# Output projection of a hybrid decoder block: when its loads are asked for, on which queue, and into which PSUM banks

## The chip, the cores and the metric

One core of a Trainium2 chip runs the whole program. The metric is device time in microseconds of one execution. Three runs of the kernel before gave 2572.22 (median), 2565.59 and 2573.88 us.

## The reference, cut to what matters

The block has 2048 tokens of width 1024, all in f32. The part that this change touches sits between the mixer's attention and the MLP:

```python
# hybrid_mixer: four gated-linear-attention heads (go), four differential-attention heads (do)
do = diff_attention(dq, dk, dv, lam)
do = from_heads(rms_norm(do, diff_norm) * (1.0 - lambda_init))
y  = jnp.concatenate([go, do], axis=-1) @ w_out          # the output projection
# reference
x = x + gt_a * rms_norm(y, post_norm_mix[l])              # residual add
h = rms_norm(x, pre_norm_mlp[l]) * (1.0 + sc_m) + sh_m    # what the MLP reads
y = jnp.square(jax.nn.relu(h @ w_up[l])) @ w_down[l]
```

## The kernel before, in words

Every f32 matrix product is made from three passes over halves: high times high, high times low, low times high. The tokens are 16 tiles of 128 rows; four tiles form a block t of 512 rows.

**Attention** (generator `attention`, lines 175 to 335) runs in two sweeps, blocks 0 and 1 first, blocks 2 and 3 second. One of its steps makes scores S for 512 keys (PSUM tag "C"), VectorE moves them out (L223, L226), ScalarE takes the exponent (L236), TensorE transposes P into PT (tag "C" too), and the product with V collects in O (tag "D"). When all four query tiles of a head and block are in, `norm` (L283) scales them into `don`, and `finish` (L296) transposes them (dps, L301), splits them into high and low halves (dmo, L303 and L304) and stores them with GpSimd's DMA queue into mixS in DRAM (L306). `finished` notes the pair (block, head).

**The output projection** (generator `out_proj`, L927) handles one token tile tk at a time. It loads mx, the tile's eight heads from mixS (1 MB, SyncE's queue, L933; two SBUF buffers), and xt, its residual rows of x (512 KB, SyncE's queue, L935; tag "wx" with three buffers, which xt shares with yt and, earlier, with the raw rows of w_out). For tk of 12 and up the load of mx is in two parts: heads 0 to 6 and head 7, so that the first part need not wait for the last head of block 3. Then come two halves b of 512 columns with 8 contraction steps k of three matmuls each (L943 to L945), so 48 matmuls of 128x512 a tile, and a `yield` after each step k. Each half collects in one PSUM bank Y. The banks have tag "A" (two banks), except for tiles 13 and 15, which use tag "C" (four banks, shared with attention's S and PT). After a half ScalarE squares it (L948). After both: the row scale, two VectorE multiplications out of PSUM into yt (L956, the last readers of Y), the residual add (L958; VectorE for tk of 11 and up, GpSimd else), the store of the new x (x1S, L959, GpSimd's queue), a second norm (L962 to L964) and the store of the normed rows (xnS, L965, GpSimd's queue).

**What sets the order.** `interleave` (L1015) advances attention by a step and then `out_proj` by 2 steps (`RA`, `RB`) or, later in the second sweep, 1.5 (`RC`), if the next tile's heads are all in `finished` (`ready`, L1034). The tiles come in the order `TOKS` (L976): 0, 4, 1, 5, 2, 6, 3, 7, 8, 9, ... 15. The first `TB` = 11 of them are woven into attention; tiles 11 to 15 follow after attention (L1157 to L1175), among the first loads of the MLP's up projection: its normed operands hsrc (`fetch_op`, L1103) and weights wA (`load_w1`, L1123), both on SyncE's queue. The lines as written are not the order on the engines, though. The program's framework builds one instruction list per engine before the run: an instruction that its plan holds ready, with a free buffer, may go ahead of others written earlier, and the earlier written goes first where several are ready. On the chip each engine and each DMA queue then keeps to its list and waits at its head.

Of the kernel before, what the change touches and what calls it, by code (L numbers as in the profile page):

```python
# [9 lines left out]
F32 = mybir.dt.float32  # L10
F32R = mybir.dt.float32r
# [8 lines left out]
P = 128  # L20
S = 2048
D = 1024
NK = D // P
NH = 4
# [10 lines left out]
AT0 = 2  # L35
GA1 = 4
WL = 2
RA = 2.0
RB = 2.0
RC = 1.5  # L40
GA0 = 22
# [8 lines left out]
def tile_hybrid_block(  # L50
# [3 lines left out]
    nc = tc.nc  # L54
# [12 lines left out]
    mixS = [dram.tile([P, 4, 2 * NH, 2, P], F32, name=f"mixS{t}") for t in range(NT)]  # L67
# [49 lines left out]
    def rsqrt_col(pool, ss, n, inv_n, tag):  # L117

        y = pool.tile([P, n], F32, tag=tag + "y", name=tag + "y", bufs=2)
        nc.scalar.activation(y, ss, AF.Ln, scale=inv_n, bias=eps_c)  # L120
        nc.scalar.activation(y, y, AF.Exp, scale=-0.5)
        v = pool.tile([P, n], F32, tag=tag + "v", name=tag + "v", bufs=2)
        nc.vector.tensor_scalar(v, ss, inv_n, EPS, op0=ALU.mult, op1=ALU.add)

        w = pool.tile([P, n], F32, tag=tag + "w", name=tag + "w", bufs=2)
        nc.vector.tensor_tensor(w, y, y, op=ALU.mult)
        nc.vector.scalar_tensor_tensor(w, w, -0.5, v, op0=ALU.mult, op1=ALU.mult)
        r = pool.tile([P, n], F32, tag=tag + "r", name=tag + "r", bufs=2)
        nc.vector.scalar_tensor_tensor(r, w, 1.5, y, op0=ALU.add, op1=ALU.mult)
        return r  # L130
# [41 lines left out]
    finished = set()  # L172
# [172 lines left out]
    pp = cps.enter_context(tc.tile_pool(name="p0ps", bufs=1, space=PSUM))  # L345
# [100 lines left out]
    def run(g, n=None):  # L446

        while n is None or n > 0:
            if next(g, run) is run:
                return False  # L450
            n = None if n is None else n - 1
        return True
# [424 lines left out]
    at = attention((0, 1), sa, 1024, 6, pp, atags, 3, 3, 2)  # L877
# [26 lines left out]
    sw = c1.enter_context(tc.tile_pool(name="p1w", bufs=2, side="left", reuse_waits="tile"))  # L904
# [4 lines left out]
    def load_wo(k):  # L909
        raw = sw.tile([P, D], F32, tag="wx", name="woraw", bufs=3)  # L910
        nc.gpsimd.dma_start(raw, w_out[k * P:(k + 1) * P, :])
        woraw.append(raw)
# [3 lines left out]
    for k in range(NK):  # L916
# [7 lines left out]
        if k + 3 < NK:  # L924
            load_wo(k + 3)

    def out_proj(tiles):  # L927

        for tk in tiles:
            assert all((tk // 4, h) in finished for h in range(NH))  # L930
            mx = sw.tile([P, 2 * NH, 2, P], F32R, tag="mx", name="mx", bufs=2)
            for ks in (slice(0, 7), slice(7, 8)) if tk >= 12 else (slice(0, 8),):
                nc.sync.dma_start(mx[:, ks].bitcast(F32), mixS[tk // 4][:, tk % 4, ks])  # L933
            xt = sw.tile([P, D], F32, tag="wx", name="wxt", bufs=3)
            nc.sync.dma_start(xt, x[tk * P:(tk + 1) * P, :])  # L935
            yps = []
            ss = sw.tile([P, 2], F32, tag="wss", name="wss", bufs=2)
            for b in range(2):
                yp = pp.tile([P, 512], F32, tag=("C" if tk > 12 and tk % 2 else "A"), name="Y",
                             bufs=4 if tk > 12 and tk % 2 else 2)  # L940
                cs = slice(512 * b, 512 * b + 512)
                for k in range(NK):
                    nc.tensor.matmul(yp, mx[:, k, 0, :], wohi[k][:, cs], start=(k == 0), stop=False)  # L943
                    nc.tensor.matmul(yp, mx[:, k, 0, :], wolo[k][:, cs], start=False, stop=False)  # L944
                    nc.tensor.matmul(yp, mx[:, k, 1, :], wohi[k][:, cs], start=False, stop=(k == NK - 1))  # L945
                    yield
                junk = sw.tile([P, 512], BF16, tag="wjunk", name="wjunk", bufs=1)
                nc.scalar.activation(junk, yp, AF.Square, accum_out=ss[:, b:b + 1])  # L948
                yps.append(yp)
            s1 = sw.tile([P, 1], F32, tag="ws1", name="ws1", bufs=2)  # L950
            nc.vector.tensor_tensor(s1, ss[:, 0:1], ss[:, 1:2], op=ALU.add)
            r = rsqrt_col(sw, s1, 1, 1.0 / D, "wr")
            yt = sw.tile([P, D], F32, tag="wx", name="wyt", bufs=3)
            for b in range(2):
                cs = slice(512 * b, 512 * b + 512)
                nc.vector.scalar_tensor_tensor(yt[:, cs], yps[b], r, gtg[:, cs], op0=ALU.mult, op1=ALU.mult)  # L956
            eng = nc.vector if tk >= 11 else nc.gpsimd
            eng.tensor_tensor(xt, xt, yt, op=ALU.add)  # L958
            nc.gpsimd.dma_start(x1S[tk], xt)  # L959

            s2 = sw.tile([P, 1], F32, tag="ws2", name="ws2", bufs=2)
            nc.scalar.activation(yt, xt, AF.Square, accum_out=s2)  # L962
            r2 = rsqrt_col(sw, s2, 1, 1.0 / D, "wq")
            nc.vector.tensor_scalar(yt, xt, r2, None, op0=ALU.mult)  # L964
            nc.gpsimd.dma_start(xnS[tk // 8][:, tk % 8], yt.rearrange("p (k c) -> p k c", c=P))  # L965
# [6 lines left out]
    wdS = [dram.tile([P, 3, 512], F32, name=f"wdS{p}") for p in range(NP_)]  # L972

    TOKS = (0, 4, 1, 5, 2, 6, 3, 7) + tuple(range(8, 16))  # L976

    def prep_first(pool, tag):


        for n in range(16):
            i, k = n // 4, n % 4
            while len(wsteps) < 32 * (i + 1) + 4:
                yield
            raw = pool.tile([P, 2, 2, P], F32, tag="prq", name="xnq", bufs=2)
            for j in range(2):
                nc.gpsimd.dma_start(raw[:, j], xnS[0][:, 4 * j + i].rearrange("p (e k) c -> p e k c", e=2)[:, :, k, :])
            for _ in range(3):
                yield
            ps = pp.tile([P, 2, 2, P], F32, tag=tag, name="ntr", bufs=4)  # L990
            for e in range(2):
                for j in range(2):
                    nc.tensor.transpose(ps[:, e, j, :], raw[:, j, e, :], ident)
            bt = pool.tile([P, 2, 2, P], F32, tag="prq", name="hBq", bufs=2)
            for e in range(2):
                kk = k + 4 * e
                nc.scalar.activation(bt[:, e], ps[:, e], AF.Identity, bias=cols[:, 24 + kk:25 + kk],
                                     scale=prem[:, 1, kk:kk + 1])
            tt = pool.tile([P, 4, P], F32, tag="prq", name="hTq", bufs=2)
            cs = slice(P * i, P * i + P)  # L1000
            b4 = bt.rearrange("p i j c -> p (i j) c")
            nc.vector.tensor_tensor(tt[:, 0:2], bt[:, :, 1, :], b4[:, 0:2], op=ALU.subtract)
            nc.vector.tensor_tensor(tt[:, 2], b4[:, 3], tt[:, 0], op=ALU.subtract)
            nc.vector.tensor_tensor(tt[:, 3], b4[:, 2], tt[:, 2], op=ALU.subtract)
            nc.gpsimd.dma_start(hS[0][:, 0, k, cs], b4[:, 0])
            nc.gpsimd.dma_start(hS[0][:, 1:3, k, cs], b4[:, 2:4])
            nc.gpsimd.dma_start(hS[0][:, 3:7, k, cs], tt)
            for _ in range(2):
                yield


    TB = 11
    op = out_proj(TOKS[:TB])

    def interleave(at, first, rate, later, pre=None):  # L1015


        due, i = 0.0, 0
        while run(at, 1):
            due += rate if i < first else later  # L1020
            while due >= 1.0:
                if len(wsteps) == 16 * TB or not ready(TOKS[len(wsteps) // 16]):
                    due = 0.0
                    break
                run(op, 1)
                wsteps.append(1)
                due -= 1.0
            if pre is not None:
                run(pre, 1)
            i += 1  # L1030

    wsteps = []

    def ready(tk):  # L1034
        return all((tk // 4, h) in finished for h in range(NH))

    interleave(at, 0, RA, RA)
    cA.close()
    cA = ExitStack()
    sa = cA.enter_context(tc.tile_pool(name="pA1", bufs=2, side="right", reuse_waits="tile"))  # L1040
    at = attention((2, 3), sa, S, 6, pp, atags, 5, 5, 2)
    pre = prep_first(sa, "C")
    interleave(at, 48, RB, RC, pre)
    run(op)
    run(pre)
# [109 lines left out]


    op = out_proj(TOKS[TB:])  # L1157
    fetch_op(0)
    run(op, 14)
# [20 lines left out]
    pp = c3.enter_context(tc.tile_pool(name="p2ps", bufs=1, space=PSUM, reuse_waits="tile"))  # L1180
# [53 lines left out]
    n = len(usteps)  # L1234
    ready_ops = {}
    prep_todo = [(k, hf) for k in range(4) for hf in range(2)]
    for s, (g, c, wi, p) in enumerate(usteps):
        i = WORD[wi]
# [17 lines left out]
        nm, first = BANK[i]  # L1256
# [34 lines left out]
    pp = c4.enter_context(tc.tile_pool(name="p3ps", bufs=1, space=PSUM, reuse_waits="tile"))  # L1291
# [157 lines left out]
    banks = {}  # L1449
# [25 lines left out]
    for s in range(nd - TAIL):  # L1475
        if s + AHEAD < nd:
            ready_ops[s + AHEAD] = down_ops(s + AHEAD)
        i, p, gs = dsteps[s]
# [98 lines left out]
```

## Time and profile before

| | |
|---|---|
| runs, us | 2572.22 median, 2565.59 to 2573.88 |
| the profiled execution's own time | 2572.86 us |
| its span, first to last instruction | 2570.7 us |
| TensorE busy | 2457.0 us, 96% of the span |
| mean granted TensorE clock | 0.982 of full speed |

The span is what the profile's rows cover, and 2.16 us lie around it. TensorE (PE) is busy nearly all the time, so time is to be had only where its rows show a pause or a lower clock. The stretch of the output projection runs from 816 us, the first of its matmuls, to 1301 us, where the up projection's matmuls begin.

### The profile page before, as it was taken

The numbers are of one execution on the slowest core, as the hardware profiler recorded it, in microseconds if no ns is written. First come the engines' busy times: TensorE is split into PE (matmuls) and PEld (weight loads), VectorE is DVE, ScalarE is ACT, GpSimd is POOL, SyncE is SP. The second block draws the span as 40 slices with busy tenths as digits, with TensorE's granted clock in tenths as the row PEclk, the third lists the DMA queues.
The fourth block names the chain that finished last, engine by engine and source line by source line (L and its number), as shares of the span: only waits on it lengthen the run. The fifth ranks groups of instructions, "written<-read, shape, count | busy, mean of one in ns | idle before, by whom it ended". The sixth has DMA issues, their size and how long they took to land.

```text
span 2570.7 us, 35387 instructions
## 1 busy us (share of the span) xinstructions
PE 2457.0 (96%) x12532; PEld 2055.5 (80%) x12532; DVE 1589.8 (62%) x3111; ACT 1159.2 (45%) x2201; POOL 417.6 (16%) x638
## 2 busy tenths in 40 slices
PE   5999999999998899999999999999999999999998
PEld 4877788887787788888778888788888788788886
DVE  7536754347865677767576667766664445544756
ACT  4352224412545566556555555544553333222444
POOL 1011230003311123232012322212211000100000
PEclk8999999999999999999999999999999999999999
DMA  7354553244845667655565655734438767855856
GB/s 270 110 191 141 179 191 111 98 141 157 242 131 181 207 206 229 204 181 158 211 224 198 232 189 175 239 134 160 157 126 301 254 198 242 279 176 161 289 167 209
DMA packets 218791, 491.60 MB, mean 191 GB/s; under 512 B 24848, under 2 KB 78800, under 8 KB 217072
## 3 DMA queue, kind: packets, MB, share of 16 engines
q1 hardware_dynamic: 170000, 329.12, 40.5%
q0 software_dynamic: 48608, 160.16, 16.8%
q8 instruction: 100, 1.64, 0.3%
q14 instruction: 83, 0.68, 0.1%
HBM read 329.79 MB, written 159.39 MB: 190 GB/s over the span
## 4 chain that ended last, share of the span: by engine, by line
issue 34%; PE 23%; POOL 7%; DVE 2%; DMA 1%; ACT 1%; POOLq 0%; SPq 0%; DVEq 0%; ACTq 0%
PE dn L1440 5%; PE dn L1441 5%; PE dn L1442 4%; PE S L218 2%; PE O L278 2%; POOL uS L1222 2%; POOL uS L1191 2%; PE Y L945 1%; PE Y L944 1%; PE Y L943 1%; PE PT L267 1%; POOL wdS L1320 1%; POOL uS L1230 1%; ACT P L236 1%; DMA q<-qS 0%
## 5 line engine op out<-in xcount | busy, mean ns | idle before, releaser
L1440 PE MATMUL dn<-dnhi,uhi 128*128 128x512 f32 x880 | 344.5, 391 | 3.0 <-DVE du L1420 3.0
L1442 PE MATMUL dn<-dnhi,ulo 128*128 128x512 f32 x880 | 344.2, 391 | 2.0 <-DVE ulo L1369 2.0
L1441 PE MATMUL dn<-dnlo,uhi 128*128 128x512 f32 x880 | 344.1, 391 | 0.0
L1367 ACT CAST uhi<-us 128x1024 fp32r<-128x1024 f32 (+1 forms) x126 | 118.7, 944 | 357.9 <-PE dn L1441 341.4
L1369 DVE TENSOR_TENSOR ulo<-us,uhi 128x1024 fp32r<-128x1024 f32 (+1 forms) x126 | 137.0, 1087 | 158.6 <-ACT uhi L1367 158.3
L535 PE MATMUL projt<-hThi,whi 128*128 128x512 f32 x512 | 203.9, 398 | 1.1 <-DVE cols L420 0.6
L537 PE MATMUL projt<-hThi,wlo 128*128 128x512 f32 x512 | 201.5, 393 | 2.2 <-DVE wlo L476 2.2
L536 PE MATMUL projt<-hTlo,whi 128*128 128x512 f32 x512 | 201.4, 393 | 0.0
L1440 PEld LDWEIGHTS dn<-dnhi,uhi 128*128 128x128 f32 x880 | 165.9, 189 | 38.9 <-ACT dnhi L1366 2.8
L1442 PEld LDWEIGHTS dn<-dnhi,ulo 128*128 128x128 f32 x880 | 165.9, 189 | 37.6 <-DVE ulo L1369 2.4
L1441 PEld LDWEIGHTS dn<-dnlo,uhi 128*128 128x128 f32 x880 | 166.0, 189 | 35.3
L236 ACT ACTIVATE P<-P,nm 128x128 f32<-128x128 f32 (+15 forms) x128 | 153.7, 1202 | 48.8 <-DVE nm L226 46.1
L1145 ACT CAST wuhi<-wA 128x512 fp32r<-128x512 f32 x160 | 99.1, 619 | 165.3 <-PE upV L1264 67.0
L218 PE MATMUL S<-K,q 128*128 128x512 f32 (+3 forms) x640 | 169.5, 383 | 2.8 <-issue 1.5
L278 PEld LDWEIGHTS O<-V,PTs 128*128 128x128 f32 x1088 | 142.3, 193 | 25.4 <-ACT PTs L269 14.3
L278 PE MATMUL O<-V,PTs 128*128 128x128 f32 x1088 | 152.6, 281 | 7.9 <-ACT PTs L269 4.2
L550 PE MATMUL projn<-whi,hThi 128*128 128x256 f32 x512 | 150.5, 294 | 4.5 <-DVE cols L420 2.7
L1265 PE MATMUL upY<-hhi,wulo 128*128 128x512 f32 x384 | 151.9, 396 | 2.0 <-DVE wulo L1146 2.0
L1263 PE MATMUL upY<-hhi,wuhi 128*128 128x512 f32 x384 | 151.7, 395 | 0.0
L1264 PE MATMUL upY<-hlo,wuhi 128*128 128x512 f32 x384 | 151.4, 394 | 0.0
L552 PE MATMUL projn<-whi,hTlo 128*128 128x256 f32 x512 | 148.1, 291 | 0.3 <-DVE hTlo L168 0.3
L551 PE MATMUL projn<-wlo,hThi 128*128 128x256 f32 x512 | 148.2, 290 | 0.0
(334 smaller groups left out, 5713.9 us busy)
## 6 DMA issues: line engine op xcount, KB each, us to landing
us<-uS SPq DMA_DIRECT2D x94, 512.0 KB, 4.4
wA<-in_w_up_dram SPq DMA_DIRECT2D x128, 256.0 KB, 3.0
uS<-t POOLq DMA_DIRECT2D x128, 256.0 KB, 3.2
wraw<-in_w_in_dram SPq DMA_DIRECT2D x48, 512.0 KB, 4.6
uS<-c POOLq DMA_DIRECT2D x96, 256.0 KB, 3.1
K<-kS SPq DMA_DIRECT2D x40, 512.0 KB, 5.5
wds<-in_w_down_dram SPq DMA_DIRECT2D x78, 256.0 KB, 4.0
adaraw<-in_ada_w_dram SPq DMA_DIRECT2D x32, 512.0 KB, 4.1
```

The lines of the kernel that those rows point to most:

```text
L218: nc.tensor.matmul(ps[:, :wd], qt[:, m, hl, qs], Kc[ci][:, m, :wd], start=(hl == 0), stop=(hl == 1))
L236: nc.scalar.activation(Ps[m][:, :width], Ps[m][:, :width], AF.Exp, scale=-1.0, bias=nms[m][:, t:t + 1], accum_out=sums[:, 0, m:m + 1])
L278: nc.tensor.matmul(outs[t, h][:, j, :], pt[:, kb % 4, :], Vc[g][:, kb % 4, :], start=(kb == 0), stop=(kb == nb - 1))
L535: nc.tensor.matmul(ps, whi[k][:, cs], hi[:, k, :], start=(k == 0), stop=False)
L536: nc.tensor.matmul(ps, whi[k][:, cs], lo[:, k, :], start=False, stop=False)
L537: nc.tensor.matmul(ps, wlo[k][:, cs], hi[:, k, :], start=False, stop=(k == NK - 1))
L1263: nc.tensor.matmul(ps, whi[:, k, :], hi[:, k, :], start=(first and k == 0), stop=False, skip_group_check=not first)
L1264: nc.tensor.matmul(ps, whi[:, k, :], lo[:, k, :], start=False, stop=False, skip_group_check=not first)
L1265: nc.tensor.matmul(ps, wlo[:, k, :], hi[:, k, :], start=False, stop=(k == 3), skip_group_check=not first)
L1440: nc.tensor.matmul(banks[t], uhi[:, tk], whi, start=first, stop=False, skip_group_check=on)
L1441: nc.tensor.matmul(banks[t], uhi[:, tk], wlo, start=False, stop=False, skip_group_check=on)
L1442: nc.tensor.matmul(banks[t], ulo[:, tk], whi, start=False, stop=last, skip_group_check=on)
```

## The change

- `load_mx(tk)` is new: it loads mx for a tile, once, and only if that tile's heads are finished. It uses SyncE's queue for tiles below 12 and GpSimd's for tiles 12 to 15, where the two parts stay (heads 0 to 6, head 7).
- In a tile's second half, after its step k = 0, the tile's own xt and the next tile's mx are asked for (`TOKS[TOKS.index(tk) + 1]`); before, both were asked for at the start of the tile they belong to.
- Tiles 11, 13 and 15 collect in "C" banks, 12 and 14 in "A". Before, 11 was in "A", and the others as now.
- `interleave` advances `out_proj` into a new tile only when its mx has been asked for, and 3 attention steps after, where it had to ask itself. The first sweep's loop is written out, with 2 steps of `out_proj` for each of attention.

```diff
+    def load_mx(tk):
+        if tk in mxs or not ready(tk):
+            return
+        mxs[tk] = sw.tile([P, 2 * NH, 2, P], F32R, tag="mx", name="mx", bufs=2)
+        eng = nc.gpsimd if tk >= 12 else nc.sync
+        for ks in (slice(0, 7), slice(7, 8)) if tk >= 12 else (slice(0, 8),):
+            eng.dma_start(mxs[tk][:, ks].bitcast(F32), mixS[tk // 4][:, tk % 4, ks])
+
     def out_proj(tiles):
         for tk in tiles:
-            assert all((tk // 4, h) in finished for h in range(NH))
-            mx = sw.tile([P, 2 * NH, 2, P], F32R, tag="mx", name="mx", bufs=2)
-            for ks in (slice(0, 7), slice(7, 8)) if tk >= 12 else (slice(0, 8),):
-                nc.sync.dma_start(mx[:, ks].bitcast(F32), mixS[tk // 4][:, tk % 4, ks])
-            xt = sw.tile([P, D], F32, tag="wx", name="wxt", bufs=3)
-            nc.sync.dma_start(xt, x[tk * P:(tk + 1) * P, :])
+            load_mx(tk)
+            mx = mxs.pop(tk)
+            banks = ("C", 4) if tk >= 11 and (tk - TB) % 2 == 0 else ("A", 2)
...
-                yp = pp.tile([P, 512], F32, tag=("C" if tk > 12 and tk % 2 else "A"), name="Y",
-                             bufs=4 if tk > 12 and tk % 2 else 2)
+                yp = pp.tile([P, 512], F32, tag=banks[0], name="Y", bufs=banks[1])
...
+                    if (b, k) == (1, 0):
+                        xt = sw.tile([P, D], F32, tag="wx", name="wxt", bufs=3)
+                        nc.sync.dma_start(xt, x[tk * P:(tk + 1) * P, :])
+                        for nx in TOKS[TOKS.index(tk) + 1:TOKS.index(tk) + 2]:
+                            load_mx(nx)
                     yield
...
+    def op_step():
+        if len(wsteps) == 16 * TB or (len(wsteps) % 16 == 0 and TOKS[len(wsteps) // 16] not in mxs):
+            return False
+        run(op, 1)
+        wsteps.append(1)
+        return True
+
-    def interleave(at, first, rate, later, pre=None):
-        due, i = 0.0, 0
+    def interleave(at, first, rate, later, pre):
+        due, i, asked = 0.0, 0, {}
         while run(at, 1):
             due += rate if i < first else later
+            n = len(wsteps) // 16
+            if len(wsteps) % 16 == 0 and n < TB and TOKS[n] not in mxs:
+                load_mx(TOKS[n])
+                asked[n] = i
             while due >= 1.0:
-                if len(wsteps) == 16 * TB or not ready(TOKS[len(wsteps) // 16]):
+                n = len(wsteps) // 16
+                if (len(wsteps) % 16 == 0 and i < asked.get(n, -3) + 3) or not op_step():
                     due = 0.0
                     break
-                run(op, 1)
-                wsteps.append(1)
                 due -= 1.0
...
-    interleave(at, 0, RA, RA)
+    load_mx(0)
+    while run(at, 1):
+        for _ in range(2):
+            op_step()
```

## Rows read from the trace of the kernel before

**Rows 1.** The page of the profile, its span and the line of TensorE: busy us, share of the span, instructions.

```profile
span 2570.7 us, 35387 instructions
...
PE 2457.0 (96%) x12532; PEld 2055.5 (80%) x12532; DVE 1589.8 (62%) x3111; ACT 1159.2 (45%) x2201; POOL 417.6 (16%) x638
```

**Rows 2.** Busy time of the engines by stretch, whole core. Columns: stretch in us, its length, busy us of PE, PEld, DVE, ACT and POOL with instructions, granted clock, share of the DMA engines, GB/s. The first two stretches are the end of attention, the other four the rest of the output projection.

```profile
1200.00:1229.00 29.00, 28.77 (x188) 24.60 (x187) 23.72 (x69) 18.53 (x36) 4.22 (x4) 1.00 0.35 114
1229.00:1249.50 20.50, 19.88 (x140) 17.53 (x138) 6.46 (x15) 12.27 (x27) 0.00 (x0) 1.00 0.00 1
1249.50:1252.90 3.40, 0.63 (x4) 0.42 (x4) 2.17 (x8) 1.31 (x5) 0.73 (x1) 0.79 0.85 272
1252.90:1258.20 5.30, 5.21 (x12) 4.12 (x13) 3.54 (x9) 2.69 (x5) 0.56 (x1) 0.50 0.98 347
1258.20:1277.60 19.40, 19.34 (x85) 15.56 (x83) 12.70 (x23) 9.17 (x19) 1.07 (x2) 1.00 1.00 374
1277.60:1301.10 23.50, 21.87 (x97) 18.14 (x98) 11.71 (x28) 7.15 (x19) 2.14 (x5) 1.00 0.81 279
```

**Rows 3.** The waits of TensorE from 790 to 1330 us: what waited, for whom, us in total, times, longest.

```profile
PE dps L301 <- DVE don L293: 8.5, 5, 6.5
PE Y L943 <- DVE wyt L956: 5.5, 3, 2.8
...
PE Y L943 <- DMA mx<-mixS: 2.4, 1, 2.4
...
PE Y L943 <- DVE ws L951: 1.7, 1, 1.7
...
PE ntr L993 <- DMA q<-qS: 1.1, 1, 1.1
```

**Rows 4.** TensorE's instructions in order of time around the last tiles: start us, busy us, engine, line, operation, tiles, shape, in brackets the pause before it and its releaser.

```profile
1248.63 0.39 PE L945 MATMUL Y<-wohi,mx 128*128 128x512 f32 x1
1249.55 0.63 PE L301 MATMUL dps<-ident,don 128*128 128x128 f32 x4 [0.54 <-DVE don L293]
1252.99 0.79 PE L943 MATMUL Y<-wohi,mx 128*128 128x512 f32 x1 [2.80 <-DVE wyt L956]
...
1277.15 0.39 PE L945 MATMUL Y<-wohi,mx 128*128 128x512 f32 x1
1279.23 0.47 PE L943 MATMUL Y<-wohi,mx 128*128 128x512 f32 x1 [1.70 <-DVE ws L951]
...
1301.08 0.39 PE L1263 MATMUL upX<-hhi,wuhi 128*128 128x512 f32 x1
```

**Rows 5.** The same stretches as in rows 2 for the instructions that write or read Y alone; columns PE, PEld, DVE, ACT, granted clock, DMA share, GB/s.

```profile
1200.00:1229.00 29.00, 5.77 (x20) 3.61 (x20) 0.31 (x1) 0.00 (x0) 1.00 0.35 114
1229.00:1249.50 20.50, 7.41 (x28) 5.04 (x28) 0.00 (x0) 1.16 (x3) 1.00 0.00 1
```

**Rows 6.** VectorE in order of time: the two readings of Y of tiles 11 and 12, after which their "A" banks are free.

```profile
1252.18 1.41 DVE L956 SCALAR_TENSOR_TENSOR wyt<-Y,wrr,gtg 128x512 f32<-128x512 f32 x2
...
1272.37 1.40 DVE L956 SCALAR_TENSOR_TENSOR wyt<-Y,wrr,gtg 128x512 f32<-128x512 f32 x2
```

**Rows 7.** SyncE's DMA queue in order of time, from the first load of mx in two parts (merged rows: us is from the first issue to the last).

```profile
1224.78 24.61 SPq L933 DMA_DIRECT2D mx<-mixS  x2
...
1260.97 0.32 SPq L933 DMA_DIRECT2D mx<-mixS  x1
...
1264.43 3.97 SPq L1123 DMA_DIRECT2D wA<-in_w_up_dram  x4
...
1269.44 1.02 SPq L1103 DMA_DIRECT2D hsrc<-hS  x2
1270.56 7.33 SPq L933 DMA_DIRECT2D mx<-mixS  x3
```

**Rows 8.** The waits of SyncE's DMA queue from 790 to 1330 us.

```profile
SPq L933 <- PE Y L945: 66.7, 8, 23.9
SPq L933 <- DMA mixS<-dmo: 52.1, 4, 15.8
...
SPq L935 <- DMA xnS<-wyt: 15.0, 2, 8.0
```

**Rows 9.** GpSimd in order of time: the last two stores of attention's heads, and the two stores of tile 11.

```profile
1221.38 0.73 POOL L306 DMA_DIRECT2D mixS<-dmo  x1 [11.06 <-DVE dmo L304]
1251.98 0.73 POOL L306 DMA_DIRECT2D mixS<-dmo  x1 [29.88 <-DVE wrw L127]
1255.14 0.56 POOL L959 DMA_DIRECT2D x1S<-wxt  x1 [2.43 <-DVE wxt L958]
1258.26 0.54 POOL L965 DMA_DIRECT2D xnS<-wyt  x1 [2.56 <-DVE wyt L964]
```

**Rows 10.** DMA issues from 1200 to 1310 us: what, queue, count, KB each, median us from issue to landing.

```profile
mx<-mixS SPq DMA_DIRECT2D x4, 896.0 KB, 5.8
```

**Rows 11.** The loads of mx that SyncE's queue issued between 860 and 1310 us, and how long they took.

```profile
L933 SPq DMA_DIRECT2D mx<-mixS x19: 319/337/430, 869.6 to 1286.4; - x19
...
DMA to landing us min/median/max: 3.4/5.8/8.9
```

**Rows 12.** ScalarE in order of time, its first pause in the up projection.

```profile
1317.01 0.59 ACT L1198 COPY p<-upX 128x512 f32<-128x512 f32 x1 [6.05 <-DMA xnS<-wyt]
```

More of the change, by code (lines that the diff above doesn't have):

```diff
@@ L37 @@
 WL = 2
-RA = 2.0
 RB = 2.0
@@ L925, in tile_hybrid_block, with ready @@
             load_wo(k + 3)
+    TOKS = (0, 4, 1, 5, 2, 6, 3, 7) + tuple(range(8, 16))
+    TB = 11
+    mxs = {}
+    def ready(tk):
+        return all((tk // 4, h) in finished for h in range(NH))
+    def load_mx(tk):
[5 more added lines that the diff above has]
+            eng.dma_start(mxs[tk][:, ks].bitcast(F32), mixS[tk // 4][:, tk % 4, ks])
     def out_proj(tiles):
         for tk in tiles:
-            assert all((tk // 4, h) in finished for h in range(NH))
-            mx = sw.tile([P, 2 * NH, 2, P], F32R, tag="mx", name="mx", bufs=2)
-            for ks in (slice(0, 7), slice(7, 8)) if tk >= 12 else (slice(0, 8),):
-                nc.sync.dma_start(mx[:, ks].bitcast(F32), mixS[tk // 4][:, tk % 4, ks])
-            xt = sw.tile([P, D], F32, tag="wx", name="wxt", bufs=3)
-            nc.sync.dma_start(xt, x[tk * P:(tk + 1) * P, :])
+            load_mx(tk)
+            mx = mxs.pop(tk)
+            banks = ("C", 4) if tk >= 11 and (tk - TB) % 2 == 0 else ("A", 2)
             yps = []
@@ L972, in tile_hybrid_block @@
     wdS = [dram.tile([P, 3, 512], F32, name=f"wdS{p}") for p in range(NP_)]
-    TOKS = (0, 4, 1, 5, 2, 6, 3, 7) + tuple(range(8, 16))
     def prep_first(pool, tag):
@@ L1009, in prep_first @@
                 yield
-    TB = 11
     op = out_proj(TOKS[:TB])
-    def interleave(at, first, rate, later, pre=None):
-        due, i = 0.0, 0
+    wsteps = []
+    def op_step():
[6 more added lines that the diff above has]
+        due, i, asked = 0.0, 0, {}
         while run(at, 1):
             due += rate if i < first else later
+            n = len(wsteps) // 16
+            if len(wsteps) % 16 == 0 and n < TB and TOKS[n] not in mxs:
+                load_mx(TOKS[n])
+                asked[n] = i
             while due >= 1.0:
-                if len(wsteps) == 16 * TB or not ready(TOKS[len(wsteps) // 16]):
+                n = len(wsteps) // 16
+                if (len(wsteps) % 16 == 0 and i < asked.get(n, -3) + 3) or not op_step():
                     due = 0.0
                     break
-                run(op, 1)
-                wsteps.append(1)
                 due -= 1.0
-            if pre is not None:
-                run(pre, 1)
+            run(pre, 1)
             i += 1
-    wsteps = []
-    def ready(tk):
-        return all((tk // 4, h) in finished for h in range(NH))
-    interleave(at, 0, RA, RA)
+    load_mx(0)
+    while run(at, 1):
+        for _ in range(2):
+            op_step()
     cA.close()
```

## The prediction

> **What bounds the kernel now.** I read the page first: TensorE is busy 2457.0 us of a span of 2570.7 [rows 1], so no more than 114 us of pauses exist in the whole program, and a change that touches only the output projection can win no more than TensorE's pauses and slow stretches there. The list of TensorE's waits between 790 and 1330 us is therefore the second view. It names five that the change could meet [rows 3]: 8.5 us in which the transposes of a head's result wait for `don`, 5.5 us in three waits for the two VectorE readings that free the "A" banks, one of 2.4 us for a load of mx, one of 1.7 us and one of 1.1 us behind a load of q. Then I read TensorE in order of time at the last tiles. Tile 11 is already drawn into attention's end: 20 of its 48 matmuls run before 1229 us and 28 until 1249.5 [rows 5], and there TensorE is busy 28.77 of 29.0 and 19.88 of 20.5 us [rows 2]. After its last matmul and the four transposes of the last head comes a pause of 2.80 us, until VectorE has read tile 11's banks [rows 4, 6]: tile 12 wants the same two "A" banks. Behind this pause the granted clock is 0.50 (1.2 GHz) for 12 matmuls in 5.30 us, then 1.00 (2.4 GHz) with 85 in 19.4 us, 0.228 us each [rows 2]. Tile 14 starts 1.70 us late at 1279.23, and at 1301.08 the up projection begins without a gap [rows 4].
>
> The 1.70 us are put down to a VectorE column sum that tile 14 does not need; its banks were free at 1273.8 [rows 6]. I put it to tile 14's mx: the buffer is free when tile 12's matmuls end at about 1265.6, but SyncE's queue first issues four loads of wA and two of hsrc and reaches it at 1270.56 [rows 7]. Landing takes up to 8.9 us [rows 11], so about 1279.
>
> **The change part by part**, against the profiled execution's own 2572.86 us (0.64 above the median of 2572.22, so the same within the runs' spread).
>
> *Banks.* Tile 11 in "C" leaves both "A" banks to tile 12, whose first seven heads are asked for at 1224.78 already [rows 7]: 42 of its 48 matmuls need neither tile 11's readings nor the last head. The pause goes: 2.80 us. Without the pause TensorE does not stop before 1258, and if the clock stays at the full level the 12 slow matmuls take 12 x 0.228 = 2.74 instead of 5.30 us: 2.56 more.
>
> What it costs: tile 11's banks now come out of attention's ring of four. No row shows Y and S sharing banks in attention's end. Bounds: 0, if a bank is free whenever TensorE has a hole there; 20 matmuls x 0.228 = 4.6 us, if tile 11 gets none before 1229, when the scores end (after that tile 12's 42 matmuls, 9.6 us, can fill instead of the 28 that fill now) [rows 2, 5]. A gain is excluded, as the holes are filled now. I take 1.0: only one bank is needed for a tile's first 24 matmuls, and the holes are where attention waits and so wants no bank itself.
>
> *GpSimd's queue.* Eight DMA issues move from SyncE's list to GpSimd's. Price of the issue: 0.53 to 0.73 us each by GpSimd's other DMAs [rows 9], 8 x 0.73 = 5.8 us at most, on an engine that the six stretches show busy for 8.7 of 101 us together [rows 2]; nobody waits for those. Tile 14's load can go when tile 12's matmuls end, 5 us earlier; with 10.9 us (48 x 0.228) until it is needed and 8.9 us at worst to land (the median of the large part is 5.8) [rows 10, 11], the 1.70 us go. What waits behind: the load of head 7 waits for the last store of heads, and behind it in GpSimd's list stand tile 11's two stores and tile 13's load. SyncE's queue reached that load only at 1260.97, 9.0 us after the store's issue at 1251.98 [rows 7, 9]. If GpSimd's list has tile 13's load behind it, that load lands at 1260.97 + 0.5 + 5.8 = 1267.3; the work left for TensorE at 1249.5, tiles 11 and 12 less what filled attention (48 matmuls, 10.9 us, and 0.6 for the transposes) ends at 1261.0. So this costs 0 to 6.3 us; I take 1.0, because the lists follow readiness: SyncE's had tile 13's load (the second of 1224.78's row) ahead of head 7's, which is written first [rows 7].
>
> The DMA engines' share is 0.98 and 1.00 at 347 and 374 GB/s in the stretches around [rows 2], so it may be the landing and not the place in the queue that makes tile 14 late; then the 1.70 us stay, a rival below. The Trainium skill (DMA: Bandwidth & Descriptors, "Issuing engines are not separate DMA queues") has a rule that speaks for that: DMAs of all queues share the same 16 engines, and a second queue saves only issue time. By that rule alone the sum would be 3.4 instead of 5.1.
>
> *Loads mid-tile, and the gating.* The lists are built by readiness, so when an mx leaves is set by its buffer, freed one tile before, not by the line: SyncE's queue stands 66.7 us in all waiting for tiles' last matmuls [rows 8]. Written half a tile earlier, the load still waits for that. xt written half a tile later may spare SyncE the 15.0 us in which it stood at xt for a "wx" buffer with loads of K, V and q behind [rows 8]; what TensorE lost to q is 1.1 us [rows 3]. Bounds 0 and 1.1; I take 0, as another wait of the same queue is likely to come last. The 2.4 us wait for mx (at 874 us) stays: the load follows the store of block 1's last head. Counting yields, 52 of the first sweep's 55 steps are past when `out_proj` begins, so 6 of its steps fall in the first loop in both kernels, every later mx is asked for by the tile before, and the delay of 3 steps never acts. The 8.5 us at `don` and the "A" waits of tiles below 11 (5.5 - 2.8 = 2.7 us) are untouched. The up projection's first pause hangs on the last tile's store [rows 12] and moves along with it.
>
> **Sum:** 2.80 + 2.56 + 1.70 = 7.1, less 1.0 and 1.0: 5.1 us. 2572.86 - 5.1 = 2567.8; less the 0.64 by which the profiled execution stands above the median, about 2567.
>
> **The rivals.** About 0.3% (7.7 us) is what a measurement of this kernel can tell from no change.
>
> *Forecast, 0.43:* the pause, the slow clock and tile 14's wait mostly go, 2564 to 2570.
>
> *The landing stays late, 0.10:* tile 14's mx comes no earlier from the other queue, because the DMA engines are full: 2.80 + 2.56 - 2.0 = 3.4, so about 2569. For: the shares of 0.98 and 1.00 [rows 2]. Against: the load leaves 5 us after its buffer is free [rows 7], and even 8.9 us of landing fit in a tile's 10.9.
>
> *It does little, 0.18:* tile 11 gets "C" banks late (4.6 us of holes), which takes most of the 7.1; 2570 to 2573. For: S and PT go through that ring until the end, and they are written earlier. Against: tile 12 can fill from about 1229.
>
> *More comes along, 0.20:* SyncE's queue no longer stands at mixS (52.1 us in four waits [rows 8]), so hsrc and wA come early, in the stretch with a DMA share of 0.00 [rows 2]; the lists come out otherwise and the 2.4, 2.7 and 1.1 us of rows 3 go too: 7.1 + 6.2 = 13.3 us, 2559 to 2564. Against: the buffers of hsrc and wA take attention's room, free only near its end.
>
> *Slower, 0.09:* GpSimd's queue becomes the wait. If tile 13's load stands behind head 7's, TensorE pauses 6.3 us at 1261 and its next 12 matmuls run at the half clock again (2.56): the 144 matmuls of tiles 13 to 15 (32.8 us) end at 1267.3 + 32.8 + 2.6 = 1302.7, 1.6 later than now. If also tile 14's and 15's loads stand behind the two stores of the tile that frees their buffer (9.2 us after its last matmul, by tile 11's 1249.0 and 1258.26 [rows 4, 9]), each comes 9.2 + 0.5 + 5.8 - 10.9 = 4.6 us late, together 10.8 us: 2583. It decides from the point where a load's place in GpSimd's list is behind a store that comes more than 5.1 us (10.9 - 5.8) after the buffer is free. Against: readiness puts such a load first, and the stores follow 6 us and more after the buffer is free.
>
> **How the numbers follow.** The likeliest case gives 2567. The faster side beyond 7.7 us, below 2564.5, has all but a little of the fourth case and a fifth of the forecast's: 0.27. Slower than 2579.9 is most of the last case: 0.07. The rest is 0.66. The range of 2556 to 2578 takes in the fourth case's sum (2559), the second and third cases and the mild end of the fifth (one load late, 2574), with some 3 us at either end for the runs' own spread (the lowest of three is 6.6 us below the median); the severe end of the fifth and larger gains stay outside.
>
> **What would show it.** Right: after the last transposes (dps, near 1249) TensorE goes on with tile 12 or 11 with no pause above 1 us and the clock at 1.00; matmuls of tile 12 stand ahead of the last head's transposes; no pause before tile 14; the last Y matmul about 5 us before 1301. Wrong: a pause of some us in the last scores with no Y in it (the ring), a pause near 1261 with GpSimd standing at head 7's load, or a pause before tile 14 that remains though its load left GpSimd early. If the time moves and the stretch from 1200 to 1301 does not, the lists elsewhere moved, and this account is wrong.

## The result, and the profile of the changed kernel

The changed kernel is a little slower. Over 20 runs of each on one chip its median is 2578.07 us against 2572.76 us, a ratio of 1.0028 with an interval of 1.0016 to 1.0041. The medians differ by 5.3 us, and the ratio puts the loss at some 7 us (4 to 11). That is inside the 0.3% that counts as no change, but on the other side of it than forecast, and just past the upper end of the range (2578). The profiled execution took 2574.04 us, near the low end of its 20 runs (2573.34 to 2591.53).

The page, its span and TensorE's line, which answer to [rows 1]:

```profile
span 2571.2 us, 35391 instructions
...
PE 2452.7 (95%) x12532; PEld 2051.5 (80%) x12532; DVE 1587.7 (62%) x3111; ACT 1157.1 (45%) x2201; POOL 420.3 (16%) x646
```

The same work as before, 4.3 us less busy, in a span 0.5 us longer: TensorE stands still about 5 us more. The waits of TensorE from 790 to 1330 us say for whom (columns as in [rows 3]):

```profile
PE dps L300 <- DVE don L292: 10.9, 6, 6.5
PE Y L955 <- DMA mx<-mixS: 8.5, 2, 5.9
...
PE Y L955 <- DVE wyt L974: 2.7, 2, 2.2
```

The wait of 2.8 us for the "A" banks and that of 1.7 us before tile 14 are gone. In their place there is one more pause at `don` and, for a load of mx, one of 5.9 us. Both stand in TensorE's instructions in order of time, as in [rows 4]:

```profile
1220.28 0.66 PE L300 MATMUL dps<-ident,don 128*128 128x128 f32 x4 [2.61 <-DVE don L292]
...
1250.70 0.63 PE L300 MATMUL dps<-ident,don 128*128 128x128 f32 x4 [0.31 <-DVE don L292]
...
1261.86 0.39 PE L957 MATMUL Y<-wohi,mx 128*128 128x512 f32 x1
...
1272.66 0.77 PE L955 MATMUL Y<-wohi,mx 128*128 128x512 f32 x1 [5.88 <-DMA mx<-mixS]
...
1307.55 0.39 PE L1287 MATMUL upX<-hhi,wuhi 128*128 128x512 f32 x1
```

To compare runs whose times are shifted I measure one stretch in all of them, from the same product of attention's end (the O row with a wait of 0.33 us for `PTs`) to the first upX matmul. Before it lasts from 1197.91 to 1301.08, 103.2 us, of which TensorE is busy 97.8; after from 1199.95 to 1307.55, 107.6 us, busy 98.2. By parts, after the change (columns as in [rows 2]):

```profile
1199.95:1229.04 29.09, 26.07 (x173) 21.87 (x174) 24.19 (x75) 20.49 (x40) 4.77 (x5) 1.00 0.31 97
1229.04:1252.00 22.96, 22.51 (x157) 19.56 (x156) 7.68 (x15) 11.98 (x25) 0.00 (x0) 1.00 0.31 114
1252.00:1266.85 14.85, 14.78 (x66) 11.88 (x64) 6.20 (x11) 6.57 (x14) 2.36 (x4) 1.00 0.54 175
1266.85:1272.66 5.81, 0.00 (x0) 0.03 (x1) 5.81 (x15) 3.57 (x10) 1.60 (x3) 0.81 1.03 406
1272.66:1280.00 7.34, 7.33 (x23) 5.94 (x24) 2.71 (x8) 0.00 (x0) 0.55 (x1) 0.69 1.02 410
1280.00:1307.55 27.55, 27.55 (x123) 22.80 (x122) 15.02 (x37) 10.54 (x28) 3.72 (x7) 1.00 0.74 258
```

Length less busy time is the time lost: 3.0 us in attention's end, where [rows 2] show 0.2 in 29 us, 0.5 in the next part, nothing around tile 12, and 5.8 in one piece before tile 13. Behind that the granted clock is 0.69 over 23 matmuls: 7.33 us where 23 x 0.228 would be 5.24, so 2.1 us (0.50, or 1.2 GHz, until about 1277, and 2.4 GHz behind it). The half clock has not gone, it has moved from tile 12 to tile 13. Instructions that touch Y alone, for [rows 5], show where the first loss begins:

```profile
1200.00:1229.00 29.00, 0.00 (x0) 0.00 (x0) 1.41 (x2) 0.00 (x0) 1.00 0.31 97
1229.00:1249.50 20.50, 6.53 (x25) 4.65 (x26) 0.00 (x0) 0.00 (x0) 1.00 0.35 128
```

Not one of the 20 matmuls that [rows 5] have before 1229 us is left. The order of TensorE's instructions says whose the later ones are (tile number, a and b its two halves of columns):

```
before: [11a]*14 dps*4 ... PT*14 [11a]*4 ... [11b]*7 ... [11b]*16 dps*4 [12a]*21 [12b]*20 [12a]*3 [12b]*4 [13a]*24 ...
after:           dps*4 ... PT*14 [12a]*3 ... [12a]*7 ... [12a]*10 [12b]*7 dps*4 [11a]*24 [11b]*24 [12a]*3 [12b]*17 [13a]*24 ...
```

Tile 11 gets its "C" bank only when attention has ended, tile 12 overtakes it, and both end within 5 us of each other. It is TensorE's list, made before the run, that holds tile 11 back, and not a bank that is still full on the chip: the last transposes of P are read out of the ring before 1244.9 us (ScalarE in order of time), and the 17 matmuls of Y that follow from 1246.27 until dps are all tile 12's. Why the plan had no bank for tile 11 before dps no run shows.

```profile
1243.82 1.07 ACT L268 COPY PTs<-PT 128x512 f32<-128x512 f32 x2 [1.93 <-PE PT L266]
```

GpSimd in order of time (compare [rows 9]) shows what follows for the loads:

```profile
1226.60 0.55 POOL L941 DMA_DIRECT2D mx<-mixS  x1 [3.14 <-PE S L217]
1253.13 0.73 POOL L305 DMA_DIRECT2D mixS<-dmo  x1 [25.97 <-DVE dmo L303]
1256.74 0.56 POOL L941 DMA_DIRECT2D mx<-mixS  x1 [2.88 <-DMA mixS<-dmo]
1263.82 1.07 POOL L941 DMA_DIRECT2D mx<-mixS  x2 [6.52 <-PE Y L957]
1267.08 1.06 POOL L941 DMA_DIRECT2D mx<-mixS  x2 [2.19 <-PE Y L957]
```

The load of head 7 (1256.74) costs the queue 2.9 us. Then GpSimd stands 6.5 us, not for a transfer but for TensorE: tile 13's load (1263.82) needs the mx buffer of tile 11, whose last matmul begins at 1261.86 (TensorE's rows above). Until then tiles 11 and 12 hold both buffers. The data land 8.7 us after the issue, at 1272.5.

### The profile page after: what moved, and what is told of

Same layout as the page of the kernel before. It is cut to its first block, busy times and chain, and to the rows that moved or that the text cites. A ratio compares the mean times of both kernels' runs of the same rounds, so it can differ in the third digit from the quotient of the medians.

```text
span 2571.2 us, 35391 instructions
## 1 busy us (share of the span) xinstructions
PE 2452.7 (95%) x12532; PEld 2051.5 (80%) x12532; DVE 1587.7 (62%) x3111; ACT 1157.1 (45%) x2201; POOL 420.3 (16%) x646
## 4 chain that ended last, share of the span: by engine, by line
PE 40%; issue 18%; DVE 3%; POOL 3%; DMA 2%; ACT 2%; POOLq 0%; DVEq 0%; SPq 0%; ACTq 0%
PE dn L1464 4%; PE dn L1466 4%; PE dn L1465 4%; PE O L277 3%; PE S L217 3%; PE upY L1289 2%; PE upY L1288 2%; PE upY L1287 2%; PE Y L955 2%; PE Y L957 2%; PE Y L956 2%; PE PT L266 1%; PE upV L1289 1%; PE upV L1288 1%; PE upV L1287 1%
```

## Experiments

The theory: from the ring of four the plan gives tile 11 no bank in attention's end, and so tiles 11 and 12 finish nearly together and keep both mx buffers. The rivals: GpSimd's queue is the wait, or the lists of attention's sweeps have changed. Every kernel was timed beside the kernel before, 1 to 4 on one chip and 5 to 8 on another, 7 to 12 runs each; the ratio to the kernel before is given with its interval. The common stretch and the rows are from one profiled execution of each.

**1. The changed kernel again**, unedited.

> The changed kernel once more, unedited, for a second profiled execution. Theory A (banks): tile 11's move to the "C" banks keeps it out of attention's end, tiles 11 and 12 then hold both mx buffers until about 1263 us, and tile 13 waits for its mx: a pause of 4 to 8 us ahead of tile 13 with a half clock behind it in this execution too, and 3 to 8 us more than the kernel before. Theory B (GpSimd's queue): the same pause, but because loads of this queue land late. Theory C (the lists of the attention sweeps changed): pauses differ from before mainly ahead of 1200 us.

2577.45 us, 1.0015 (1.0005 to 1.0024): the loss is there again. By the ratio it is about half the first (3.9 us against 7.2), by the medians nearly the same (4.8 against 5.3); together some 4 to 7 us. Both pauses return, in TensorE's order of time:

```profile
1223.40 1.11 PE L300 MATMUL dps<-ident,don 128*128 128x128 f32 x4 [2.62 <-DVE don L292]
...
1276.24 0.76 PE L955 MATMUL Y<-wohi,mx 128*128 128x512 f32 x1 [5.24 <-DMA mx<-mixS]
```

The common stretch takes 108.3 us.

**2. The banks alone**, in the kernel before:

```diff
-                 yp = pp.tile([P, 512], F32, tag=("C" if tk > 12 and tk % 2 else "A"), name="Y",
-                              bufs=4 if tk > 12 and tk % 2 else 2)
+                 yp = pp.tile([P, 512], F32, tag=("C" if tk >= 11 and tk % 2 else "A"), name="Y",
+                              bufs=4 if tk >= 11 and tk % 2 else 2)
```

> The kernel before with the new bank choice alone: tiles 11, 13 and 15 in "C", 12 and 14 in "A"; loads, queues and weaving as before. Theory A: slower than before by 3 to 8 us, with no matmul of tile 11 ahead of attention's end and a pause of 4 to 8 us ahead of tile 13, on SyncE's queue now. Theory B: no loss, 0 to 5 us faster, as the pause at tile 12 is gone and the loads stay on SyncE's queue. Theory C: within 2 us of before.

2576.44 us, 1.0014 (1.0003 to 1.0025), stretch 107.1 us. All mx loads are on SyncE's queue here, and the loss is the same. TensorE in order of time:

```profile
1221.24 1.11 PE L301 MATMUL dps<-ident,don 128*128 128x128 f32 x4 [2.62 <-DVE don L293]
...
1271.49 0.47 PE L943 MATMUL Y<-wohi,mx 128*128 128x512 f32 x1 [2.76 <-DMA mx<-mixS]
...
1286.11 0.47 PE L943 MATMUL Y<-wohi,mx 128*128 128x512 f32 x1 [1.85 <-DVE wqw L127]
```

The pause at `don` comes with the banks, and so does a late load of tile 13, with no load on GpSimd's queue at all. The pause before it is shorter than expected (2.76 us, not 4 to 8). SyncE's queue asks for tile 13's heads when tile 11's last matmul frees the buffer, and for tile 14's behind an xt that leaves at 1280.24, some 12 us after tile 12's last matmul; tile 14 pauses 1.85 us, as it paused 1.70 before, when its load stood behind wA and hsrc:

```profile
1264.22 0.80 SPq L933 DMA_DIRECT2D mx<-mixS  x2
...
1280.66 0.86 SPq L933 DMA_DIRECT2D mx<-mixS  x2
```

GpSimd's queue is not needed for the loss.

**3. Everything but the banks**, the changed kernel with the banks of before:

```diff
-             banks = ("C", 4) if tk >= 11 and (tk - TB) % 2 == 0 else ("A", 2)
+             banks = ("C", 4) if tk > 12 and tk % 2 else ("A", 2)
```

> The changed kernel with the old bank choice: 11, 12 and 14 in "A", 13 and 15 in "C"; loads mid-tile, GpSimd's queue and the new weaving stay. Theory A: between 6 us faster than before and equal: tile 11 fills attention's end again (48 matmuls ahead of 1250 us), the pause of about 2.8 us at tile 12 and its half clock stay, the 1.7 us ahead of tile 14 go. Theory B: slower than before by 3 to 8 us, with tile 13 or 14 waiting for mx. Theory C: slower than before by 3 to 8 us, with the loss ahead of 1200 us.

2568.85 us, 0.9978 (0.9967 to 0.9990), stretch 101.3 us: the other half of the change is a gain, of some 4 us by the medians and 6 by the ratio (3 to 8). TensorE in order of time, and the stretch behind the pause by engines (columns as in [rows 2]):

```profile
1257.47 0.80 PE L955 MATMUL Y<-wohi,mx 128*128 128x512 f32 x1 [2.81 <-DVE wyt L974]
```

```profile
1257.47:1262.80 5.33, 5.33 (x13) 4.17 (x14) 3.57 (x8) 2.59 (x5) 1.78 (x3) 0.50 0.49 196
```

The pause at tile 12 and its half clock are those of [rows 2, 4]. No wait for mx is left, neither at tile 13 nor at tile 14: the stretch is shorter by 1.9 us, about the 1.70 of tile 14.

**4. The two rings exchanged**: 11, 13 and 15 in "A", 12 and 14 in "C". Then attention's end keeps its filling and tile 12 still has banks of its own.

```diff
-             banks = ("C", 4) if tk >= 11 and (tk - TB) % 2 == 0 else ("A", 2)
+             banks = ("C", 4) if tk >= 12 and (tk - TB) % 2 == 1 else ("A", 2)
```

> The changed kernel with the two rings swapped for the last tiles: 11, 13 and 15 in "A", 12 and 14 in "C". Theory A: 4 to 9 us faster than before: tile 11 fills attention's end from "A", tile 12 starts in "C" right behind the last transposes with no pause, and no tile waits for mx. Theory B: no faster than e3 by more than 2 us, with tile 13 waiting for mx. Theory C: as e3, slower than before by 3 to 8 us.

2568.77 us, 0.9986 (0.9976 to 0.9997), stretch 101.6 us: a gain of some 4 us, at the low end of what was expected. TensorE in order of time:

```profile
1261.02 0.50 PE L955 MATMUL Y<-wohi,mx 128*128 128x512 f32 x1 [1.29 <-DMA mx<-mixS]
...
1300.16 0.77 PE L1287 MATMUL upX<-hhi,wuhi 128*128 128x512 f32 x1 [4.17 <-DVE wyt L974]
```

The last Y matmul ends 97.4 us into the stretch (1296.0 less 1198.55), between 5 and 6 us sooner than before. Not expected were the 1.29 us in tile 12, until head 7's load lands. Then 4.2 us go back: tile 15 is in "A" here, and the up projection's first tile must wait for its readings.

**5. Tile 15 in "C" as well**, so that no tile follows another on "A" directly and the up projection finds its banks free:

```diff
-             banks = ("C", 4) if tk >= 11 and (tk - TB) % 2 == 0 else ("A", 2)
+             banks = ("C", 4) if tk in (12, 14, 15) else ("A", 2)
```

> The changed kernel with tiles 12, 14 and 15 in "C" and 11 and 13 in "A". In e4 the output projection ended 5 us earlier than before, and the up projection then waited 4.2 us for the readings of tile 15's "A" banks. Theory A, with that second wait taken away (tile 15 in "C"): 5 to 9 us faster than the kernel before, up projection starting within 1 us of tile 15's last matmul near 1296 us. Rival (the banks only move the pause): a wait of 2 to 5 us elsewhere between 1250 and 1340 us, and no better than e4 (2 to 5 us faster).

2565.78 us, 0.9978 (0.9965 to 0.9991): faster than the kernel before, and so than the changed one, which is slower. The whole stretch by engines, and TensorE in order of time:

```profile
1204.68:1302.20 97.52, 95.08 (x535) 80.55 (x536) 62.95 (x157) 53.98 (x116) 13.28 (x21) 1.00 0.59 208
```

```profile
1267.38 0.50 PE L955 MATMUL Y<-wohi,mx 128*128 128x512 f32 x1 [1.53 <-DMA mx<-mixS]
...
1302.20 0.39 PE L1287 MATMUL upX<-hhi,wuhi 128*128 128x512 f32 x1
```

97.5 us where the kernel before needs 103.2: 3.0 us fewer pauses (2.4 against 5.4) and 2.7 fewer busy, as the clock is 1.00 throughout. The pause of 1.53 us stands inside tile 12, until head 7's load lands. Whether it beats experiment 3 in the whole time, the two intervals do not say; in the stretch it is 3.7 us shorter.

**6. Experiment 5 with every load of mx on SyncE's queue:**

```diff
-         eng = nc.gpsimd if tk >= 12 else nc.sync
+         eng = nc.sync
```

> As e5, but every load of mx stays on SyncE's queue. If GpSimd's queue is worth what the prediction gave it (tile 14's wait of 1.7 us): 1 to 4 us slower than e5, with a pause for mx ahead of tile 13 or 14. If the queue is worth nothing: within 1 us of e5.

2570.69 us, 0.9994 (0.9982 to 1.0007): not to be told from the kernel before. Stretch 100.3 us. TensorE, and SyncE's queue in order of time:

```profile
1271.12 0.50 PE L955 MATMUL Y<-wohi,mx 128*128 128x512 f32 x1 [2.89 <-DMA mx<-mixS]
...
1283.66 0.47 PE L955 MATMUL Y<-wohi,mx 128*128 128x512 f32 x1 [1.14 <-DMA mx<-mixS]
```

```profile
1232.14 24.61 SPq L941 DMA_DIRECT2D mx<-mixS  x2
1256.92 0.33 SPq L961 DMA_DIRECT2D wxt<-in_x_dram  x1
1257.35 1.08 SPq L1127 DMA_DIRECT2D hsrc<-hS  x2
1267.30 0.32 SPq L941 DMA_DIRECT2D mx<-mixS  x1
```

The shorter pause is the expected one: tile 14's load leaves at 1276.05, behind eight loads of wA and an xt, some 3 us after tile 12's last matmul. The longer one stands in tile 12, until head 7's load lands. That load leaves 8.0 us after the store of the last head (issued at 1259.35); in experiment 5 it leaves GpSimd 5.3 us after it (1258.79). What it waits for is the landing of the store. How long that took (DMA issues, as in [rows 10]), first here and then in experiment 5:

```profile
mixS<-dmo POOLq DMA_DIRECT2D x1, 512.0 KB, 7.9
...
mixS<-dmo POOLq DMA_DIRECT2D x1, 512.0 KB, 4.8
```

The engines in these two stretches (columns as in [rows 2]):

```profile
1259.35:1267.28 7.93, 7.93 (x37) 6.57 (x36) 5.41 (x10) 2.70 (x5) 1.82 (x3) 1.00 1.00 357
...
1258.79:1263.58 4.79, 4.79 (x23) 3.97 (x22) 3.10 (x6) 1.83 (x5) 1.09 (x2) 1.00 0.61 240
```

The DMA engines' share is 1.00 here and 0.61 there. Here SyncE's queue has stood for 24 us at tile 13's load, which waits for its buffer, and lets xt and hsrc go only just before the store. In experiment 5 that load stands on GpSimd, and the first three loads of hsrc have gone 20 us and more before:

```profile
1231.84 5.96 SPq L1127 DMA_DIRECT2D hsrc<-hS  x3
...
1264.13 1.30 POOL L941 DMA_DIRECT2D mx<-mixS  x2 [0.35 <-issue]
```

The other traces agree: the store lands in 9.0 and 8.4 us at a share of 1.00 in the kernel before and in experiment 8, where SyncE stands in the same way, and in 3.3 to 4.8 us at 0.44 to 0.63 in the rest. No run takes away these loads alone, so that they delay the store is a reading of the rows. The other queue is worth 2.8 us in the stretch and 4.9 between the medians. So the rival had the sign of the queue wrong.

**7. No load of tile 13.** The changed kernel without this load: tile 13 is multiplied from tile 12's heads, and everything else stays.

```diff
+         if tk == 13:
+             mxs[tk] = mx12[0]
+             return
          mxs[tk] = sw.tile([P, 2 * NH, 2, P], F32R, tag="mx", name="mx", bufs=2)
+         if tk == 12:
+             mx12.append(mxs[tk])
```

> The changed kernel without the load of tile 13's mx: tile 13 multiplies tile 12's heads a second time (that load and tile 13's own heads are left out). If the loss ahead of tile 13 is the load that finds both buffers taken by tiles 11 and 12: no pause ahead of tile 13, no half clock behind it, and 6 to 9 us faster than the changed kernel, so 2 to 5 us faster than the kernel before. If the loss lies in attention's end alone (tile 11 kept out of it, some 3 us) or elsewhere: within 2 us of the changed kernel.

2570.32 us, 0.9990 (0.9976 to 1.0003): not to be told from the kernel before, and below the changed kernel's 2577 to 2578. Stretch 100.3 us, 7.3 less than with the load. The waits of TensorE from 1190 to 1335 us:

```profile
PE dps L300 <- DVE don L292: 2.9, 2, 2.6
...
PE Y L960 <- DVE wyt L979: 0.7, 1, 0.7
```

No pause before tile 13 and no slow matmuls behind it; the pause at `don` stays. So the late load is 7 us of the loss (5.8 pause and 2.1 clock in the table above, less the 0.7 that is left here), and the filling that is missing in attention's end another 2.6 to 2.8. Why the load is late this run does not say; GpSimd's wait for tile 11's last matmul does (the rows of the changed kernel).

**8. Experiment 5's banks with the loads of before**, in the kernel before:

```diff
-                 yp = pp.tile([P, 512], F32, tag=("C" if tk > 12 and tk % 2 else "A"), name="Y",
-                              bufs=4 if tk > 12 and tk % 2 else 2)
+                 yp = pp.tile([P, 512], F32, tag=("C" if tk in (12, 14, 15) else "A"), name="Y",
+                              bufs=4 if tk in (12, 14, 15) else 2)
```

> The kernel before with e5's banks alone: 12, 14 and 15 in "C", 11 and 13 in "A"; loads at the start of their tile on SyncE's queue, old weaving. If the banks carry the gain: 3 to 7 us faster than before. If the loads mid-tile and GpSimd's queue carry it: within 2 us of before, with waits for mx ahead of tiles 13 and 14.

2573.78 us, 1.0007 (0.9993 to 1.0020): not to be told from the kernel before. Stretch 103.8 us. TensorE in order of time:

```profile
1267.87 0.50 PE L943 MATMUL Y<-wohi,mx 128*128 128x512 f32 x1 [1.53 <-DMA mx<-mixS]
...
1282.09 0.63 PE L943 MATMUL Y<-wohi,mx 128*128 128x512 f32 x1 [4.22 <-DMA mx<-mixS]
```

The pause for tile 12's banks goes; one of 1.53 us for head 7's load comes inside the tile, and tile 14's load, still where SyncE's queue has it, is late by 4.2 us instead of 1.7. Good banks alone gain nothing: TensorE reaches the next late load sooner.

## Why the prediction was wrong, by its own steps

- **Banks, what they bring (2.80 + 2.56): right, for another tile's sake.** In the changed kernel no pause stands between 1250.7 and 1266.85 and the clock there is 1.00. Experiments 3 and 5, which differ in the banks alone, show what is left of it where the loads keep up: 3.7 us of stretch, as the pause of 2.81 and 2.5 us of slow clock go and 1.53 us come in for head 7's load.
- **Banks, what they cost (1.0, bounds 0 to 4.6): this step failed.** Two reasons were given for a value near zero: one bank is enough for 24 matmuls, and the holes are where attention wants no bank. Tile 11 got no bank at all before 1229 us, and none until dps: the upper bound's own case, with the prediction's own sign of it, a pause in the last scores with no Y in it. The direct price, 2.8 us, still lies within the bounds. The price that the step did not have is behind it. The bound said that tile 12's matmuls "can fill instead"; they did (the order of instructions), and this reverses the two tiles. Before, tile 11's matmuls end at 1249.0 and free a buffer some 16 us ahead of tile 13's start; after, they end near 1262.2, 4.6 us ahead of tile 12's end, and a load that leaves 1.6 us later and lands in 8.7 does not fit. 5.8 us of pause and 2.1 of half clock: that is the 7 us of experiment 7. With the 2.8 the banks cost about 10 us, more than twice the upper bound.
- **GpSimd's queue, tile 14's 1.70 us: right.** There is no pause before tile 14, and in experiment 3 none for mx at all.
- **GpSimd's queue, what it costs (1.0, bounds 0 to 6.3): mis-sized.** Head 7's load holds GpSimd for 2.9 us, and tile 13's load behind it waits for TensorE 6.5 us more, so nothing is lost by the place in the queue. The 9.0 us that the prediction took for the time until SyncE's queue reached head 7's load were the landing of the store; in the changed kernel it took 3.3 us, and the load left 3.6 us after the store's issue. Between experiments 5 and 6 the queue is a gain of 2.8 us: about 1.1 of it the pause before tile 14 (the term above), 1.4 the pause for head 7's load. Here the rule of the Trainium skill (DMA: Bandwidth & Descriptors, "Issuing engines are not separate DMA queues") that was weighed before can be judged. That the transfers share their engines agrees: the share is 1.02 and more from 1266.85 to 1280 us with the loads of mx on GpSimd's queue and 0.98 and 1.00 before with them on SyncE's [rows 2], and from the other queue they land no sooner, but later, in a median 7.6 us for the large part against 5.8 [rows 10] (DMA issues of the changed kernel from 1200 to 1310 us):

```profile
mx<-mixS POOLq DMA_DIRECT2D x4, 896.0 KB, 7.6
```

  That a second issuing engine saves only the time to issue does not: eight issues at 0.32 us on SyncE's queue would be 2.6 us of that queue's time, off TensorE's path. What was saved is the standing of loads behind one that waits: tile 14's behind others, and hsrc behind tile 13's, until it met the store that head 7 needed.
- **Loads mid-tile (0): too low, by a little.** With the queue taken off (experiment 6), loads and banks together win 2.9 us of stretch over the kernel before, and the same banks with the loads of before lose 0.7 (experiment 8): 3.5 us are due to the new order of loads on SyncE's queue, or to the new weaving, which goes with it. I cannot split this between xt, the loads of mx and what follows them.
- **The rival "slower" had the place, the price and the half clock, and the wrong cause.** It put a pause of 6.3 us at 1261 before tile 13 and 2.56 of half clock behind it; measured are 5.88 us, which ends at 1272.66, and 2.1. Its mechanism, a load behind head 7's in GpSimd's list, is refuted by experiment 2 (same loss, no such queue) and by GpSimd's own rows: head 7's load is gone at 1256.74, and the 6.5 us behind it are a wait for TensorE. With the true mechanism the chance of 0.09 would have been far too small: the bound of 4.6 us, which I held unlikely, decides both.
- **The sum.** 5.1 us of gain were forecast; the stretch got 4.4 us longer. Against the terms: 7.1 won as forecast, 2.8 lost in attention's end, 5.8 before tile 13 and 2.1 in it make 3.6 us longer; 0.8 is not placed. Experiment 5, where tile 11 stays in "A", comes near the sum (5.7 us shorter), in part by luck: pause, slow clock and tile 14's wait go as forecast, but the 2.0 us taken off for the ring and the queue were not what was lost there; that was 1.53 us for head 7's load.
- **What the stretch does not explain.** In the profiled execution SyncE asks for hsrc from 1226.30 instead of 1249.98, the up projection's first pause shrinks, and from the first upX to the last it takes 615.7 us against 620.8. But this part takes 614.4 to 618.8 in the eight experiments, whatever they change, and the down projection 605.8 to 611.3 (before 608.6), so I put no cause to it. It is why the profiled executions differ by 1.2 us only. The attention sweeps before the stretch take 381.5 us before and 382.2 to 383.8 in the kernels where I measured them (after and experiments 1 to 4), gains and losses alike: the changed lists there do not part the two. That the changed kernel's 20 runs spread over 18 us, those before over 15, stays open.

A third mx buffer would have been the most direct test of the theory. It was not tried.

## What to carry to other kernels

When work that fills another stage's holes is given banks out of that stage's own ring, ask first when the plan will give it one; if the scheduler then fills with the next piece instead, follow the reversed order to every buffer that the two pieces hold, and to the load that waits for it. Before giving a tile other banks, look at both neighbours, the one that it takes banks from and the one that finds them occupied (the up projection here), and move the loads in the same step: here the good banks without the loads gave nothing, and the loads without the banks a third of what both gave in the stretch. A load that waits for data or for a buffer keeps back all that stands behind it in its queue (24 us at tile 13's load in experiment 6), and what it keeps back may then leave together with a store that another load needs. A second queue is worth those waits, not the time of the issues.

## What was not expected of the hardware

Pauses of the same length left two different clocks. Behind the pause of 2.81 us in experiment 3 the granted clock is 0.50 (1.2 GHz) for 13 matmuls, but behind that of 2.89 us in experiment 6 it is 1.00 (2.4 GHz). In experiment 3 a pause of 0.52 us and only 0.63 us of work stand just ahead of it. But what TensorE did ahead of the pause doesn't part two other cases: in experiment 2 it was busy without a gap for 16.1 us, paused for 2.76 us, and ran at 0.56; in experiment 6 it was busy without a gap for 11.3 us, paused for 2.89, and kept the full clock. First experiment 2, by stretches (PE alone: length, busy us, granted clock, DMA share, GB/s), then experiment 6 behind its pause (columns as in [rows 2]):

```profile
1255.00:1268.73 13.73, 13.73 (x61) 1.00 0.65 219
1268.73:1271.49 2.76, 0.00 (x1) 1.00 1.01 389
1271.49:1275.00 3.51, 3.51 (x9) 0.56 1.03 372
```

```profile
1271.12:1274.00 2.88, 2.88 (x13) 2.38 (x14) 0.22 (x1) 1.88 (x4) 0.00 (x0) 1.00 0.93 322
```

The pauses of 1.29 and 1.53 us in experiments 4 and 5 cost no clock; those of 4.17, 4.22, 5.24 and 5.88 us (experiments 4, 8 and 1, and the changed kernel) did: 0.50 to 0.53 in the first 2 to 3 us behind them. In between, a pause of nearly 3 us costs either nothing behind it (experiment 6) or 1.5 to 2.4 us (experiments 2 and 3, against 0.228 us a matmul), and what decides was not found.
